# One order for VectorE and ScalarE through a whole MLP, and block products taken by pairs of tiles

## The chip, the core and the metric

The kernel runs on one core of one Trainium2 chip. The metric is the device time of one execution in microseconds (us), taken as the median of several runs. All engine names are those of the profile: PE is the matrix engine TensorE, PEld its weight loads, DVE is VectorE, ACT is ScalarE, POOL is GpSimd, and SP is the engine that issues most transfers (DMAs).

## What is computed

One layer of a hybrid decoder on a sequence of 512 tokens with 1024 channels, in float32. Three token mixers come first (an attention, a pooling and a gated MLP), then an output projection, a norm and a residual. The change touches only what follows them, the channel MLP:

```python
h = rms_norm(x, g_ff_pre[l])
ff = jnp.square(jax.nn.relu(h @ w_ff_in[l])) @ w_ff_out[l]     # 1024 -> 4096 -> 1024
x = x + rms_norm(ff, g_ff_post[l])
```

## The kernel before

**Precision.** Every matrix operand is held as a high and a low part. ACT casts the high part, DVE subtracts it from the original to get the low part, and PE makes three matmuls of each product: high by high, low by high, high by low. A weight arrives as a chunk of 128x1024 in a buffer `raw` (three of them), ACT casts it to `whi`, DVE writes `wlo` (six of each). `split_chunk` (L188) does this for one chunk, and starts the load of the chunk that is three further on. A `Weights` object (L232) calls it when a product asks for a weight: it makes all chunks ready up to three ahead of the one asked for.

**The MLP** goes through the 4096 hidden channels in four blocks (`b`, L961) of 1024. In each block, `ff_in` makes eight hidden tiles of 128 channels by 512 tokens (tile `accf`, 24 matmuls each), and `ff_act` (L898) takes ReLU (`rl`) and square (`ec`) on ACT, splits them (`ah`, `al`) and, for every second hidden tile, makes four more sums (`ec<-ec`, DVE) and splits those too; that second split is put off until `rest()` (L893) is called, by the next `ff_act` or ahead of the products.

**The products.** The second matrix product of the block is made by a scheme that needs seven products of half-size blocks instead of eight, in four stages named s2, s1, s3 and s4. Tokens come in four tiles t of 128; p is 0 or 1, and tiles p and 2 + p make a pair. M = 4 counts the pairs of hidden tiles. The banks of PSUM are `accy` (stage s2, and the product with the part A22), `accx` (A11, then AN, then AS, added up one on the other) and `accz` (AQ, then AR), each for p = 0 and 1. `gather` (L933) adds a bank to the result `ys` on DVE (in the first block the first such step of each `ys` is a copy on ACT). `accx` is gathered after A11, after AN, and after AS; since the next part is added in the same bank, PE can't go on there until DVE has read it. The weights of s1, s3 and s4 are sums of blocks of `w_ff_out`, which DVE makes in `block_sums` (L217) ahead of the cast. Four chunks make up each of s1, s3 and s4, and two s2; a chunk of s1, s3 or s4 feeds twelve matmuls.

In the three blocks that aren't the last, s3 first makes all of AN and gathers it, then all of AS, and s4 takes AR and A22 by turns. The last block goes by token tiles so that tiles finish one after another: each is scaled (`scaled_out`, L941), its squares are summed on ACT (`junk`), and `finish_out` (L948) multiplies it by its norm factor, adds the residual `x1b`, and stores it. For token tile 2 ACT and POOL do this (`pool=True`).

**What sets the order.** `InOrder` (L80) wraps an engine. While its flag `on` is true, each instruction is tied to the one before it on that engine, so the engine runs them as the program emits them. While it is false, a scheduler chooses the order by its own estimate of times. PE and SP go through the wrapper as well; PE is always tied. L982 switches DVE and ACT to the scheduler early in the first block, L1077 switches them back shortly before the end.

Of the kernel before, what the change touches and what calls it, by code (L numbers as in the profile page):

```python
# [48 lines left out]
def trunk_layer(ctx: ExitStack, tc: tile.TileContext, x, w_in, w_pool, pool_scale, gm_gain,  # L49
# [108 lines left out]
    NB = 4  # L158
    FT = FF // P // NB
    for b in range(NB):  # L160
        for f in range(0, FT, 2):
            use["f1", b, f] = plan_cols(ff_in_k, (b * FT + f) * P)


        for stage in ("s2", "s1", "s3", "s4"):
            use[stage, b] = range(len(plan), len(plan) + (2 if stage == "s2" else FT // 2))
            for m in range(0, FT // 2, 2 if stage == "s2" else 1):
                b11, b12, b21, b22 = (
                    ff_out_k[:, b * FT + 2 * m + o:b * FT + 2 * m + o + 1, c:c + 512]
                    for o in range(2) for c in (0, 512))  # L170
                if stage == "s2":
                    plan.append([ff_out_k[:, b * FT + 2 * m + 1:b * FT + 2 * m + 4:2, :512]])
                else:
                    plan.append({"s1": [b11, b12], "s3": [b22, b12], "s4": [b22, b21]}[stage])
                    derive[len(plan) - 1] = (stage, m)

    loaded, made = [], []

# [38 lines left out]
    def block_sums(raw, stage, m):  # L217

        one, two = raw[:, :512], raw[:, 512:]
        if stage == "s1":  # L220
            t1s[m] = ff.tile([P, T], F32, name="t1", bufs=4)
            dve.tensor_add(t1s[m], one, two)
            return [one, t1s[m]]
        if stage == "s3":

            dve.tensor_add(t1s[m], t1s[m], one)
            dve.tensor_add(two, two, one)
            return [t1s[m], two]
        dve.tensor_add(two, two, t1s[m])
        return [raw]  # L230

    class Weights:  # L232
# [697 lines left out]
    def block(which, p):  # L930
        return psum.tile([P, T], F32, name="acc" + which, tag=which, bufs=2)
# [13 lines left out]
            yg[t][hf] = slot("tmp", "yg") if t == LAST else ys[t][hf]  # L945
        dve.tensor_mul(yg[t][hf][:, c], ys[t][hf][:, c], gfpost[hf][:, c])

    def finish_out(t, r, g, c=WHOLE, queue=None, pool=False):  # L948

        rows = slice(t * P, (t + 1) * P)  # L950
        at = slice(g * T + c.start, g * T + c.stop)
        y = yg[t][g][:, c]
        if pool:
            act.activation(y, y, AF.Copy, scale=r)
            nc.gpsimd.tensor_add(y, y, x1b[t][:, at])
        else:
            dve.scalar_tensor_tensor(y, y, r, x1b[t][:, at], ALU.mult, ALU.add)
        (queue or nc.sync).dma_start(o2[rows, at], y)

    M = FT // 2  # L960
    for b in range(NB):  # L961
        first = 0
        if b == 0:

            first = 4
            halves = slice(0, T // 2), slice(T // 2, T)
            wks = [Weights(("f1", b, f), ahead=2 - f) for f in (0, 2)]
            pss = [bank4("mm", f, "psf") for f in range(first)]
            for f in range(first):
                ff_in(pss[f], wks[f // 2], f % 2, halves[0],  # L970
                      (lambda f=f: turn(f)) if f >= 2 else None)
            early.close()
            ff = ctx.enter_context(tc.tile_pool(name="ff", bufs=1, reuse_waits="tile"))
            home[0] = ff
            RINGS["tmp"] = 4
            gfpost = bcast_row(g_ff_post[0], [ff.tile([P, T], F32, name=f"gfpost{g}")
                                              for g in range(2)])
            Weights(("f1", b, first), ahead=2)[0]
            for f in range(first):
                ff_in(pss[f], wks[f // 2], f % 2, halves[1])  # L980
                ff_act(f, pss[f])
            act.on = dve.on = False  # L982
            banks.close()
            psum = ctx.enter_context(tc.tile_pool(name="psum2", bufs=1, space=PSUM,
                                                  reuse_waits="tile"))
            z = [block("z", p) for p in range(2)]
        for f in range(first, FT):
            if f % 2 == 0:
                wk = Weights(("f1", b, f))
            ps = block("f", f)  # L990
            ff_in(ps, wk, f % 2, slice(0, T))
            ff_act(f, ps)
        final = b == NB - 1
        if final:
            for i in range(2):
                pair = ff.tile([P, 2, D], F32, name="x1b", tag="ec", bufs=2)
                for t in (2 * i, 2 * i + 1):
                    x1b[t] = pair[:, t - 2 * i, :]
                    sp.dma_start(x1b[t], x1d[t])

        def stage(name, n, keep=False):

            wk = Weights((name, b), keep=keep)
            wk.tiles = [(i, j, k) for i in use[name, b] for j in range(len(plan[i]))
                        for k in range(plan[i][j].shape[1])]
            return lambda m, j: tile_of(wk, m * n + j)

        def tile_of(wk, i):
            i, j, k = wk.tiles[i]
            wk.ready(i)  # L1010
            h, l = made[i][j]
            return h[:, k, :], l[:, k, :]

        two = range(2)

        stagger = (0, 0), (0, 1), (1, 0), (0, 2), (1, 1), (0, 3), (1, 2), (1, 3)
        y = [block("y", p) for p in two]
        x = [block("x", p) for p in two]
        if b:
            z = [block("z", p) for p in two]  # L1020
        w2, w1 = stage("s2", 1, True), stage("s1", 2)
        def first(m, j):
            for p in two:
                product((x, z)[j][p], (A11, AQ)[j], p, m, w1(m, j))

        rest()
        for m in range(M):
            if m == M - 1:

                first(0, 0)  # L1030
                first(0, 1)
            for p in two:
                product(y[p], A12, p, m, w2(m, 0))
        for p in two:
            gather(2 + p, 0, y[p], ALU.add, b)
        for m, j in (1, 0), (1, 1), (2, 0), (3, 0), (2, 1), (3, 1):
            first(m, j)
            if (m, j) == (3, 0):
                for p in two:
                    gather(2 + p, 0, x[p], ALU.add, b)  # L1040
        if final:
            for p in two:
                scaled_out(2 + p, 0)
        for p in two:
            gather(p, 1, z[p], ALU.add, b)
        w = stage("s3", 2, True)
        for p, m in stagger:
            product(x[p], AN, p, m, w(m, 0), False)
            if m == M - 1:
                gather(2 + p, 1, x[p], ALU.subtract, b)  # L1050
        for p in two:
            for m in range(M):
                product(x[p], AS, p, m, w(m, 1), False)
            gather(p, 1, x[p], ALU.subtract, b)
            gather(p, 0, x[p], ALU.add, b)
        y = [block("y", p) for p in two]
        w = stage("s4", 2, final)
        if not final:
            for m in range(M):
                for j, ps, part in (0, z, AR), (1, y, A22):  # L1060
                    for p in two:
                        product(ps[p], part, p, m, w(m, j), j == 1)
            for p in two:
                gather(2 + p, 1, z[p], ALU.add, b)
                gather(p, 0, y[p], ALU.add, b)
            continue
        for p in two:
            scaled_out(p, 1)
        r = {}
        for p, m in stagger:  # L1070
            product(z[p], AR, p, m, w(m, 0), False)
            if m == M - 1:
                gather(2 + p, 1, z[p], ALU.add, b)
                scaled_out(2 + p, 1)
                r[2 + p] = post_r(2 + p)

        act.on = dve.on = True  # L1077
        for m in range(M):
            product(y[0], A22, 0, m, w(m, 1), True)
        gather(0, 0, y[0], ALU.add, b)  # L1080
        scaled_out(0, 0)
        for g in two:
            finish_out(2, r[2], g, pool=True)
        r[0] = post_r(0)
        finish_out(3, r[3], 1)
        for c in HALVES:
            ps = block("f", 0) if c.start else y[1]
            for m in range(M):
                product(ps, A22, 1, m, w(m, 1), True, c)
            gather(1, 0, ps, ALU.add, b, c)  # L1090
            scaled_out(1, 0, c)
        finish_out(3, r[3], 0)
        r[1] = rstd_d(twos[1], "p")
        for g in two:
            finish_out(0, r[0], g)
        finish_out(1, r[1], 1, queue=nc.scalar)
        finish_out(1, r[1], 0, HALVES[0])
        finish_out(1, r[1], 0, HALVES[1], queue=nc.scalar)


_INS = ["x", "w_in", "w_pool", "pool_scale", "gm_gain", "w_spatial", "b_spatial", "w_br_sb",
# [26 lines left out]
```

## Time and profile before

| what | value |
|---|---|
| median of 3 runs | 726.25 us (725.29 to 728.44) |
| the profiled execution's own time | 729.78 us |
| its span, first to last instruction | 728.0 us |
| PE busy | 703.2 us, 97% of the span |
| DVE busy | 495.4 us, 68% |
| ACT busy | 355.1 us, 49% |

The profiled execution is 3.5 us above the median and 1.8 us longer than its span. Busy time tells which engine has the most to do; what a change is worth is told by which engine waits for which, and where.

### The profile page before, as it was taken

To read this page: it belongs to the slowest core of one execution; us is meant where nothing else is said; L and a number is where in the kernel's file an instruction comes from. 1 tells how busy PE (TensorE), PEld (TensorE's weight loads), DVE (VectorE), ACT (ScalarE), POOL (GpSimd) and SP (SyncE) were. 2 spreads that over 40 slices of the span, in tenths; PEclk is the share of its full clock that TensorE was granted. 3 is DMA by queue.
4 is the path that set the end of the run, shared out by engine and by line. 5 is a ranking of instruction groups with operands and counts; after the bars stand their busy time and mean duration, and the time that the engine had idled before them with its cause. 6 is when DMAs were issued, how large, how long until landed. Compare 5 with 4: busy or idle time off the path is not lost.

```text
span 728.0 us, 9146 instructions
## 1 busy us (share of the span) xinstructions
PE 703.2 (97%) x3320; PEld 580.3 (80%) x3320; DVE 495.4 (68%) x769; ACT 355.1 (49%) x595; POOL 57.5 (8%) x108
## 2 busy tenths in 40 slices
PE   7999999999999999999999998999999999999984
PEld 4889887787888888888899776888878887888863
DVE  6745799777777444342676776656975678757876
ACT  6566656655544333321456564455434553455522
POOL 4100222111121000000030000000000000000003
PEclk9999999999999999999999999999999999999997
DMA  7272312322224332261336334732456225633623
GB/s 273 77 209 83 115 59 59 91 77 66 87 58 145 90 113 88 91 227 59 115 91 200 115 99 133 228 104 86 144 177 187 86 88 175 206 112 108 203 95 116
DMA packets 72431, 89.80 MB, mean 123 GB/s; under 512 B 4545, under 2 KB 49729, under 8 KB 72386
## 3 DMA queue, kind: packets, MB, share of 16 engines
q1 hardware_dynamic: 72096, 88.82, 39.3%
q8 instruction: 26, 0.43, 0.3%
q10 hardware_dynamic: 290, 0.40, 0.1%
q14 instruction: 19, 0.16, 0.1%
HBM read 85.01 MB, written 4.19 MB: 123 GB/s over the span
## 4 chain that ended last, share of the span: by engine, by line
PE 74%; DVE 13%; DMA 8%; ACT 2%; issue 2%; SPq 0%; POOL 0%; DVEq 0%; ACTq 0%; POOLq 0%
PE psc L90 26%; PE accf L90 16%; DMA raw<-in_w_ff_out_dram 7%; PE psb L90 6%; PE acc L90 6%; PE accx L90 4%; DVE wlo L90 3%; PE psv L90 3%; PE accz L90 3%; PE accy L90 3%; DVE ys L90 2%; PE psgv L90 2%; DVE raw L90 1%; PE z L90 1%; DVE t L90 1%
## 5 line engine op out<-in xcount | busy, mean ns | idle before, releaser
L90 DVE TENSOR_TENSOR wlo<-raw,whi 128x1024 fp32r<-128x1024 f32 (+1 forms) x145 | 159.1, 1101 | 106.8 <-ACT whi L90 106.1
L90 ACT CAST whi<-raw 128x1024 fp32r<-128x1024 f32 (+1 forms) x152 | 139.4, 927 | 141.2 <-PE psc L90 31.1
L90 PE MATMUL psc<-hT,whi 128*128 128x512 f32 x576 | 182.1, 397 | 0.0
L90 PE MATMUL accf<-hT,whi 128*128 128x512 f32 x448 | 138.1, 389 | 1.8 <-ACT rl L90 1.8
L90 PEld LDWEIGHTS psc<-hT,whi 128*128 128x128 f32 x576 | 103.8, 188 | 21.0 <-issue 1.5
L90 PE MATMUL psc<-hT,wlo 128*128 128x512 f32 x288 | 112.5, 391 | 0.0
L90 PEld LDWEIGHTS accf<-hT,whi 128*128 128x128 f32 x448 | 83.9, 188 | 19.6 <-ACT rl L90 2.2
L90 PE MATMUL accf<-hT,wlo 128*128 128x512 f32 x224 | 87.1, 389 | 0.0
L90 PEld LDWEIGHTS psc<-hT,wlo 128*128 128x128 f32 x288 | 54.1, 188 | 11.7
L90 PEld LDWEIGHTS accf<-hT,wlo 128*128 128x128 f32 x224 | 42.0, 188 | 8.7
L90 ACT CAST ah<-ec 128x768 fp32r<-128x768 f32 (+1 forms) x32 | 30.2, 944 | 37.6 <-DVE ec L90 37.1
L90 PE MATMUL accx<-whi,ah 128*128 128x512 f32 x96 | 39.1, 408 | 6.5 <-DVE ys L90 6.5
L284 POOL TENSOR_TENSOR pr<-pv,mhalf 128x1 f32<-128x1 f32 x8 | 5.6, 699 | 471.6 <-DVE pv L90 471.6
L90 PE MATMUL accx<-whi,al 128*128 128x512 f32 x96 | 38.8, 404 | 0.0
L90 PE MATMUL accx<-wlo,ah 128*128 128x512 f32 x96 | 38.7, 403 | 0.0
L90 DVE TENSOR_TENSOR al<-ec,ah 128x768 fp32r<-128x768 f32 (+1 forms) x32 | 34.8, 1088 | 4.5 <-ACT ah L90 4.5
L90 DVE TENSOR_TENSOR_SCAN nb<-nb,zeros 128x128 f32<-128x128 f32 (+3 forms) x32 | 27.5, 863 | 7.5 <-POOL nb L482 7.1
L90 DVE TENSOR_TENSOR ec<-ec 128x256 f32<-128x256 f32 x64 | 26.7, 421 | 7.2 <-ACT ec L90 6.9
L90 PEld LDWEIGHTS accx<-whi,ah 128*128 128x128 f32 x96 | 18.9, 197 | 12.6 <-DVE ys L90 8.6
L90 ACT CAST whi<-t 128x512 fp32r<-128x512 f32 x32 | 19.7, 617 | 14.7 <-PE accz L90 6.9
L90 ACT CAST a<-pt 128x128 fp32r<-128x128 f32 (+3 forms) x32 | 13.6, 426 | 25.9 <-PE pt L90 25.8
L90 ACT ACTIVATE sg<-psc 128x512 f32<-128x512 f32 x24 | 14.3, 597 | 22.7 <-PE psc L90 22.7
(199 smaller groups left out, 1251.7 us busy)
## 6 DMA issues: line engine op xcount, KB each, us to landing
raw<-in_w_ff_out_dram SPq DMA_DIRECT2D x96, 256.0 KB, 3.2
raw<-in_w_in_dram SPq DMA_DIRECT2D x42, 512.0 KB, 3.8
raw<-in_w_ff_in_dram SPq DMA_DIRECT2D x32, 512.0 KB, 3.9
xt<-in_x_dram SPq DMA_DIRECT2D x16, 256.0 KB, 5.8
raw<-in_w_out_dram SPq DMA_DIRECT2D x8, 512.0 KB, 3.7
raw<-in_w_ff_out_dram SPq DMA_DIRECT2D x8, 512.0 KB, 4.6
raw<-in_w_br_sb_dram SPq DMA_DIRECT2D x4, 512.0 KB, 3.5
x1d<-xt SPq DMA_DIRECT2D x8, 256.0 KB, 2.8
```

The costliest lines, as they stand in the source:

```text
L90: i = op(*args, **kw).ins
L284: nc.gpsimd.tensor_tensor(r, v, mhalf, ALU.pow)
```

## The change

Three things change, all in the MLP.

1. The two lines that switch the wrapper's flag off and on again are gone, so DVE and ACT keep the order of the program from the output projection to the end.
2. In the first three blocks, s3 takes A22 (`accy`) and AN (`accx`) by turns, and s4 takes AR (`accz`) and AS (`accx`) by turns, always two tiles p at a time. The blocks of weights move between the stages to fit, and in s3 both halves of a chunk are now summed in place and cast in one instruction of 128x1024 instead of two of 128x512. The number of sums is the same.
3. In the last block the two store steps of token tile 2 move from ACT and POOL to DVE, the last steps are in another order, and all weights of s4 are asked for before its first product.

```diff
-                    plan.append({"s1": [b11, b12], "s3": [b22, b12], "s4": [b22, b21]}[stage])
-                    derive[len(plan) - 1] = (stage, m)
+                    kind = stage + "f" * (b == NB - 1 and stage != "s1")
+                    plan.append({"s1": [b11, b12], "s3": [b22, b21], "s4": [b12, b22],
+                                 "s3f": [b22, b12], "s4f": [b22, b21]}[kind])
+                    derive[len(plan) - 1] = (kind, m)
...
         if stage == "s3":
+            dve.tensor_add(one, one, t1s[m])
+            dve.tensor_add(two, two, one)
+        elif stage == "s4":
+            dve.tensor_add(one, one, two)
+        elif stage == "s3f":
             dve.tensor_add(t1s[m], t1s[m], one)
             dve.tensor_add(two, two, one)
             return [t1s[m], two]
-        dve.tensor_add(two, two, t1s[m])
+        else:
+            dve.tensor_add(two, two, t1s[m])
         return [raw]
...
-            act.on = dve.on = False
...
+        if not final:
+            w = stage("s3", 2)
+            for m in range(M):
+                for j, ps, part in ((0, x, AN), (1, y, A22))[::1 if m == M - 1 else -1]:
+                    for p in two:
+                        product(ps[p], part, p, m, w(m, j), j == 1)
+                    if m == M - 1:
+                        for p in two:
+                            gather(*((p, 0, y[p], ALU.add, b) if j else
+                                     (2 + p, 1, x[p], ALU.subtract, b)))
+            w = stage("s4", 2)
+            for m in range(M):
+                for j, ps, part in (1, z, AR), (0, x, AS):
+                    for p in two:
+                        product(ps[p], part, p, m, w(m, j), False)
+            for p in two:
+                gather(2 + p, 1, z[p], ALU.add, b)
+            for p in two:
+                gather(p, 1, x[p], ALU.subtract, b)
+                gather(p, 0, x[p], ALU.add, b)
+            continue
...
-        w = stage("s4", 2, final)
-        if not final:
-            for m in range(M):
-                for j, ps, part in (0, z, AR), (1, y, A22):
-                    for p in two:
-                        product(ps[p], part, p, m, w(m, j), j == 1)
-            for p in two:
-                gather(2 + p, 1, z[p], ALU.add, b)
-                gather(p, 0, y[p], ALU.add, b)
-            continue
+        w = stage("s4", 2, True)
+        for m in range(M):
+            w(m, 0)
...
-        act.on = dve.on = True
         for m in range(M):
             product(y[0], A22, 0, m, w(m, 1), True)
         gather(0, 0, y[0], ALU.add, b)
+        finish_out(2, r[2], 0)
         scaled_out(0, 0)
-        for g in two:
-            finish_out(2, r[2], g, pool=True)
```

How the instructions of DVE move is seen at three places, all in the second block; the third block reads the same. The names are tiles with their numbers: `raw` a chunk, `t1` the running sum of two blocks of weights, `ec` and `al` hidden tiles, `ys` the result.

The first place is where the block's last hidden tiles (`ec_4663` before, `ec_4655` after) meet the first chunks of s1. On DVE before:

```order
L90 TENSOR_TENSOR wlo_4641<-raw_4544,whi_4640 128x512
L90 TENSOR_TENSOR wlo_4641<-t1_4642,whi_4640 128x512
L90 TENSOR_TENSOR wlo_4714<-raw_4563,whi_4713 128x512
L90 TENSOR_TENSOR wlo_4714<-t1_4715,whi_4713 128x512
L90 TENSOR_TENSOR t1_4755<-raw_4648 128x512
L90 TENSOR_TENSOR ec_4578<-ec_4578 128x256 x2
L90 TENSOR_TENSOR al_4613<-ec_4578,ah_4612 128x768
L90 TENSOR_TENSOR t1_4642<-t1_4642,raw_4721 128x512
L90 TENSOR_TENSOR ec_4578<-ec_4578 128x256
L90 TENSOR_TENSOR raw_4721<-raw_4721 128x512
L90 TENSOR_TENSOR al_4613<-ec_4578,ah_4612 128x1024
L90 TENSOR_TENSOR ec_4663<-ec_4663 128x256
```

On DVE after:

```order
L90 TENSOR_TENSOR t1_4634<-raw_4536 128x512
L90 TENSOR_TENSOR wlo_4633<-raw_4536,whi_4632 128x512
L90 TENSOR_TENSOR wlo_4633<-t1_4634,whi_4632 128x512
L90 TENSOR_TENSOR al_4605<-ec_4570,ah_4604 128x1024
L90 TENSOR_TENSOR al_4690<-ec_4655,ah_4689 128x768
L90 TENSOR_TENSOR ec_4655<-ec_4655 128x256 x4
L90 TENSOR_TENSOR al_4690<-ec_4655,ah_4689 128x1024
L90 TENSOR_TENSOR t1_4707<-raw_4555 128x512
L90 TENSOR_TENSOR wlo_4706<-raw_4555,whi_4705 128x512
L90 TENSOR_TENSOR wlo_4706<-t1_4707,whi_4705 128x512
L90 TENSOR_TENSOR t1_4730<-raw_4617 128x512
L90 TENSOR_TENSOR wlo_4729<-raw_4617,whi_4728 128x512
```

Before, the second chunk of s1 (`wlo_4714`) and sums for later chunks stand ahead of the last hidden tiles; after, the second chunk (`wlo_4706`) stands behind both splits of the last hidden tiles.

The second place is the start of s3, up to the gather that frees `accx` for AN. On DVE before:

```order
L90 TENSOR_TENSOR wlo_4785<-t1_4642,whi_4784 128x512
L90 TENSOR_TENSOR raw_4761<-raw_4761 128x512
L90 TENSOR_TENSOR wlo_4785<-raw_4721,whi_4784 128x512
L90 TENSOR_TENSOR ec_4663<-ec_4663 128x256
L90 TENSOR_TENSOR ys_4134<-ys_4134,accy_4705 128x512
L90 TENSOR_TENSOR wlo_4808<-t1_4715,whi_4807 128x512
L90 TENSOR_TENSOR wlo_4808<-raw_4744,whi_4807 128x512
L90 TENSOR_TENSOR ys_4136<-ys_4136,accy_4706 128x512
L90 TENSOR_TENSOR al_4698<-ec_4663,ah_4697 128x1024
```

On DVE after:

```order
L90 TENSOR_TENSOR ys_4136<-ys_4136,accy_4698 128x512
L90 TENSOR_TENSOR raw_4713<-raw_4713,t1_4634 128x512
L90 TENSOR_TENSOR raw_4713<-raw_4713 128x512
L90 TENSOR_TENSOR wlo_4777<-raw_4713,whi_4776 128x1024
L90 TENSOR_TENSOR raw_4736<-raw_4736,t1_4707 128x512
L90 TENSOR_TENSOR raw_4736<-raw_4736 128x512
L90 TENSOR_TENSOR wlo_4798<-raw_4736,whi_4797 128x1024
L90 TENSOR_TENSOR raw_4753<-raw_4753,t1_4730 128x512
L90 TENSOR_TENSOR raw_4753<-raw_4753 128x512
L90 TENSOR_TENSOR wlo_4813<-raw_4753,whi_4812 128x1024
L90 TENSOR_TENSOR ys_4134<-ys_4134,accx_4699 128x512
```

Before, other work stands between a chunk's sums and its `wlo`; after, each chunk's two sums are followed by its own `wlo`, and the first gather of `accx` comes behind three chunks of s3.

The third place is the gather that frees `accx` for AS. On DVE before:

```order
L90 TENSOR_TENSOR raw_4832<-raw_4832,t1_4715 128x512
L90 TENSOR_TENSOR raw_4865<-raw_4865,t1_4738 128x512
L90 TENSOR_TENSOR ys_4257<-ys_4257,accx_4707 128x512
L90 TENSOR_TENSOR wlo_4886<-raw_4832,whi_4885 128x1024
L90 TENSOR_TENSOR raw_4876<-raw_4876,t1_4755 128x512
L90 TENSOR_TENSOR ys_4265<-ys_4265,accx_4708 128x512
```

On DVE after:

```order
L90 TENSOR_TENSOR wlo_4846<-raw_4782,whi_4845 128x1024
L90 TENSOR_TENSOR raw_4803<-raw_4803 128x512
L90 TENSOR_TENSOR wlo_4867<-raw_4803,whi_4866 128x1024
L90 TENSOR_TENSOR raw_4818<-raw_4818 128x512
L90 TENSOR_TENSOR wlo_4887<-raw_4818,whi_4886 128x1024
L90 TENSOR_TENSOR raw_4851<-raw_4851 128x512
L90 TENSOR_TENSOR wlo_4906<-raw_4851,whi_4905 128x1024
L90 TENSOR_TENSOR ys_4282<-ys_4282,accx_4699 128x512
L90 TENSOR_TENSOR ys_4284<-ys_4284,accx_4700 128x512
L90 TENSOR_TENSOR ys_4292<-ys_4292,accy_4843 128x512
```

After, the fourth chunk of s3 (`wlo_4846`) and three chunks of s4 stand ahead of this gather; before, it stood between single steps of the s4 chunks.

## Rows read from the trace of the kernel before

**Rows 1.** The page: the span.

```profile
span 728.0 us, 9146 instructions
```

**Rows 2.** Windows: length, busy PE, PEld, DVE, ACT, POOL (count), clock, DMA share, GB/s.

```profile
421.80:465.40 43.60, 40.30 (x169) 32.55 (x169) 30.22 (x42) 23.08 (x34) 0.00 (x0) 0.96 0.48 146
465.40:508.90 43.50, 43.50 (x193) 36.04 (x192) 28.23 (x41) 23.02 (x32) 0.00 (x0) 1.00 0.39 121
508.90:547.70 38.80, 38.44 (x170) 31.49 (x169) 32.09 (x46) 16.97 (x23) 0.00 (x0) 1.00 0.54 163
...
591.20:630.40 39.20, 38.73 (x170) 31.37 (x169) 32.29 (x46) 17.37 (x23) 0.00 (x0) 1.00 0.53 163
...
673.90:717.30 43.40, 40.33 (x181) 33.12 (x179) 34.77 (x57) 18.76 (x34) 1.77 (x3) 0.96 0.36 121
717.30:728.00 10.70, 0.00 (x0) 0.00 (x0) 7.20 (x15) 1.02 (x4) 3.93 (x4) 0.61 0.52 196
```

**Rows 3.** Waits of PE in the MLP: for whom, us in total, times, longest.

```profile
PE accx L90 <- DVE ys L90: 6.5, 5, 3.0
PE accf L90 <- ACT rl L90: 1.8, 1, 1.8
```

**Rows 4.** Timeline of DVE, second block's products: start, duration, instruction, idle before.

```profile
512.79 0.95 DVE L90 TENSOR_TENSOR al<-ec,ah 128x768 fp32r<-128x768 f32 x1
...
514.26 0.42 DVE L90 TENSOR_TENSOR ec<-ec 128x256 f32<-128x256 f32 x1
514.60 0.69 DVE L90 TENSOR_TENSOR wlo<-t,whi 128x512 fp32r<-128x512 f32 x1
...
519.14 1.22 DVE L90 TENSOR_TENSOR al<-ec,ah 128x1024 fp32r<-128x1024 f32 x1
...
523.89 1.28 DVE L90 TENSOR_TENSOR ys<-ys,accx 128x512 f32<-128x512 f32 x2
```

**Rows 5.** Timelines of ACT and DVE: hidden tiles' chain, and sum to cast.

```profile
503.68 1.06 ACT L90 CAST ah<-ec 128x1024 fp32r<-128x1024 f32 x1 [2.49 <-DVE ec L90]
...
509.95 0.59 ACT L90 ACTIVATE rl<-accf 128x512 f32<-128x512 f32 x1
...
511.24 0.84 ACT L90 CAST ah<-ec 128x768 fp32r<-128x768 f32 x1
511.98 0.61 ACT L90 CAST whi<-t 128x512 fp32r<-128x512 f32 x1
...
694.11 1.05 ACT L90 CAST whi<-raw 128x1024 fp32r<-128x1024 f32 x1 [2.73 <-DVE raw L90]
...
504.77 1.23 DVE L90 TENSOR_TENSOR al<-ec,ah 128x1024 fp32r<-128x1024 f32 x1 [0.52 <-ACT ah L90]
...
693.34 0.69 DVE L90 TENSOR_TENSOR raw<-raw,t 128x512 f32<-128x512 f32 x1 [1.51 <-DMA raw<-in_w_ff_out_dram]
```

**Rows 6.** Timelines of DVE and PE at the longest wait, last block.

```profile
697.49 0.68 DVE L90 TENSOR_TENSOR raw<-raw,t 128x512 f32<-128x512 f32 x1
698.09 0.68 DVE L90 TENSOR_TENSOR ys<-ys,accx 128x512 f32<-128x512 f32 x1
...
698.82 0.54 PE L90 MATMUL accx<-whi,ah 128*128 128x512 f32 x1 [3.00 <-DVE ys L90]
```

**Rows 7.** Windows behind the 1.8 us wait and the 3.0 us wait, columns as in rows 2.

```profile
410.80:414.00 3.20, 3.17 (x14) 2.64 (x15) 3.12 (x6) 3.19 (x6) 0.00 (x0) 1.00 0.07 23
...
699.20:702.60 3.40, 3.40 (x10) 2.63 (x9) 1.99 (x3) 0.00 (x0) 0.00 (x0) 0.51 0.32 122
```

**Rows 8.** Loads of `w_ff_out` chunks (median us to landing), and of `x1b`.

```profile
raw<-in_w_ff_out_dram SPq DMA_DIRECT2D x96, 256.0 KB, 3.2
...
DMA to landing us min/median/max: 5.2/6.0/6.9
```

**Rows 9.** Timelines of DVE and POOL behind the last matmul.

```profile
719.71 1.04 DVE L90 TENSOR_TENSOR yg<-ys,gfpost 128x256 f32<-128x256 f32 x1
...
718.93 1.53 POOL L955 TENSOR_TENSOR ys<-ys,x1b 128x512 f32<-128x512 f32 x1
```

More of the change, by code (lines that the diff above doesn't have):

```diff
@@ L946, in scaled_out, with finish_out @@
         dve.tensor_mul(yg[t][hf][:, c], ys[t][hf][:, c], gfpost[hf][:, c])
-    def finish_out(t, r, g, c=WHOLE, queue=None, pool=False):
+    def finish_out(t, r, g, c=WHOLE, queue=None):
         rows = slice(t * P, (t + 1) * P)
@@ L952, in finish_out @@
         y = yg[t][g][:, c]
[L953 to L957, printed above, removed]
+        dve.scalar_tensor_tensor(y, y, r, x1b[t][:, at], ALU.mult, ALU.add)
         (queue or nc.sync).dma_start(o2[rows, at], y)
@@ L1040, in trunk_layer @@
                     gather(2 + p, 0, x[p], ALU.add, b)
-        if final:
-            for p in two:
-                scaled_out(2 + p, 0)
         for p in two:
             gather(p, 1, z[p], ALU.add, b)
+        y = [block("y", p) for p in two]
+        if not final:
[19 more added lines that the diff above has]
+            continue
+        for p in two:
+            scaled_out(2 + p, 0)
         w = stage("s3", 2, True)
@@ L1055, in trunk_layer @@
             gather(p, 0, x[p], ALU.add, b)
-        y = [block("y", p) for p in two]
-        w = stage("s4", 2, final)
-        if not final:
-            for m in range(M):
-                for j, ps, part in (0, z, AR), (1, y, A22):
-                    for p in two:
-                        product(ps[p], part, p, m, w(m, j), j == 1)
-            for p in two:
-                gather(2 + p, 1, z[p], ALU.add, b)
-                gather(p, 0, y[p], ALU.add, b)
-            continue
+        w = stage("s4", 2, True)
+        for m in range(M):
+            w(m, 0)
         for p in two:
@@ L1074, in trunk_layer @@
                 scaled_out(2 + p, 1)
-                r[2 + p] = post_r(2 + p)
-        act.on = dve.on = True
+        for p in two:
+            r[2 + p] = post_r(2 + p)
         for m in range(M):
@@ L1080, in trunk_layer @@
         gather(0, 0, y[0], ALU.add, b)
+        finish_out(2, r[2], 0)
         scaled_out(0, 0)
-        for g in two:
-            finish_out(2, r[2], g, pool=True)
-        r[0] = post_r(0)
-        finish_out(3, r[3], 1)
         for c in HALVES:
@@ L1089, in trunk_layer @@
                 product(ps, A22, 1, m, w(m, 1), True, c)
+            if c.start:
+                finish_out(2, r[2], 1)
             gather(1, 0, ps, ALU.add, b, c)
             scaled_out(1, 0, c)
+            if not c.start:
+                r[0] = post_r(0)
         finish_out(3, r[3], 0)
         r[1] = rstd_d(twos[1], "p")
[L1094 to L1098, printed above, removed]
+        finish_out(3, r[3], 1)
+        finish_out(0, r[0], 1)
+        finish_out(0, r[0], 0, queue=nc.scalar)
+        finish_out(1, r[1], 1)
+        finish_out(1, r[1], 0, HALVES[0], queue=nc.scalar)
+        finish_out(1, r[1], 0, HALVES[1])
 _INS = ["x", "w_in", "w_pool", "pool_scale", "gm_gain", "w_spatial", "b_spatial", "w_br_sb",
```

## The prediction, made before the changed kernel ran

> **What bounds the kernel now.** I read the MLP by stages first. The hidden tiles of a block take 43.5 us for 192 matmuls with PE busy throughout, 0.2266 us a matmul; the 168 matmuls of a product stage should then take 38.1. The four product stages take 43.6, 38.8, 39.2 and 43.4 [rows 2], so the two in the middle are within about 1 us of PE's pace. The waits say what is lost: 6.5 us in five waits of `accx` for a gather, and 1.8 for a ReLU [rows 3]. At the longest one DVE was not idle: a sum for a later chunk stood ahead of the gather, and PE started 0.05 us after the gather's end [rows 6]. Behind that 3.0 us wait PE ran 3.4 us at a granted clock of 0.51, the 1.2 GHz level, a loss of 3.4 x 0.49 = 1.7; behind the 1.8 us wait it stayed at 1.00 [rows 7]. That happened twice (both outer stages show 0.96 [rows 2]). So at most 8.3 + 3.3 = 11.6 us can come back from PE's waits, in 726.
>
> DVE is the engine to look at, since it is busy for 32 of the middle stages' 39 us [rows 2]. What counts is when it reaches a gather.
>
> **What the change does to DVE: prices.** Back to back, DVE starts each instruction 0.08 before the last record ends (two gathers in 1.28 [rows 4]), so I count 0.60 for a sum, a gather or a 512-wide subtraction, 0.34 for an `ec` step, 0.87 and 1.14 for `al` 768 and 1024 wide, and 1.14 for a 1024-wide `wlo`, which has no row here and the same shape as that `al` [rows 4]. From the end of a sum to its cast 0.08 passes, from the end of a cast to DVE 0.03; casts take 0.61, 0.84 and 1.05 for 512, 768 and 1024 [rows 5].
>
> A chunk needs sums (DVE), cast (ACT), subtraction (DVE). In the scheduler's order other work fills DVE while ACT casts. In the program's order the next instruction on DVE is the subtraction that waits for this cast. A chunk of the new s3 then holds DVE for 0.60 + 0.69 + 0.08 + 1.05 + 0.03 + 1.14 = 3.59 us, one of s4 (one sum) for 2.99, one of s1 for 0.69 + 0.08 + 0.61 + 0.03 + 0.60 = 2.01. PE uses up a chunk in 12 x 0.2266 = 2.72. The single wide cast saves little: two subtractions are 1.20, one is 1.14. It also takes away an overlap, since with two casts the first subtraction can run under the second.
>
> The Trainium skill (Perfetto Trace Analysis, section Per-instruction lifecycle) says that ACT, DVE and GpSimd are strict FIFOs, so a ready gather can't pass a waiting subtraction. Rows 6 agree. By that rule the sum is the one below; without it a gather would go when its bank is ready, and the time would be that of rival 1.
>
> **The walk through block two.** Time 0 is the stage's first `accy` matmul.
> - The last hidden tiles come first now: ReLU at about 0.2 (estimate), 1.29 to the cast, 0.84, `al` 768 to 3.2, four sums to 4.7, cast 1024 to 5.8, `al` 1024 to 7.0 [rows 4, 5].
> - Chunks two to four of s1, 3 x 2.01, to 13.0, each just ahead of PE (8.2, 10.9 and 12.2). Two gathers of `accy`, 14.2.
> - Three chunks of s3, 3 x 3.59, to 25.0. Only then comes the gather of `accx`; PE may go on at 25.7. PE finished s1 (72 matmuls) at 16.3 and, with the first chunk ready at 17.8, `accy` at 19.1. It waits 6.6 us. Before, the same gather ran at 523.89 [rows 4], 15.0 after the stage's start.
> - Three more gathers to 27.4, the fourth chunk of s3 to 31.0, three of s4 to 40.0: behind these stands the gather that frees `accx` for AS, done at 40.7. PE had finished s3 and the first AR at 36.5, and waits 4.2.
> - Then 42 matmuls, 9.5: the stage ends at **50.2** instead of 38.8 (+11.4). Block three is the same: +11.0.
>
> A chunk's load takes 3.2 [rows 8] and a buffer is free two chunks, 6 us or more, ahead of its next use, so loads don't hold this up.
>
> Block one: its first gathers of `accy`, `accz` and (in s3) `accx` are copies on ACT. Three s3 chunks end at 23.8, two gathers 25.0, the fourth chunk 28.6, two s4 chunks 34.5; sum and cast of the third to 36.4 stand ahead of the copy on ACT, 37.0; plus 9.5 is 46.5 against 43.6: +2.9. Ahead of it, ACT's order no longer puts a cast before the ReLU that PE waited 1.8 for [rows 3]: -1.8.
>
> Block four keeps its stages. Its s3 chunks are still cast in halves (2.61 each), but start when `raw` has landed behind the 2 MB of `x1b`: 9.0 + 6.5 = 15.6 (median and maximum for `x1b` are 6.0 and 6.9 [rows 8]). Three chunks to 23.4, the `accx` gather 24.1, others and two scalings to 27.0, the fourth chunk 29.6, two s4 chunks 35.6, and only then the gather for AS, 36.4. AS of p = 0 to 39.1, p = 1 to 41.8, gathers to 43.1, and behind these, in order, the last two s4 chunks to 46.1 and 49.1. AR ends at 51.0; A22 (12 whole and 24 half-wide matmuls) takes 5.4: **56.5** against 43.4, +13.1.
>
> **The end.** The last 10.7 us have no matmul [rows 2]. A DVE step of 256 columns took 1.04 there while POOL ran its add [rows 9]; elsewhere such a step takes 0.42. Without POOL that goes, and two 512-wide steps come to DVE; in the new order I count 9.4 from the last matmul to the end: -1.3, bounds 0 and -3.
>
> **The clock.** Waits of 4 to 8 us come back in three stages in a place where PE is what everything then waits for; behind 3.0 us the loss was 1.7 [rows 7]. 3 x 1.7 = +5.0, bounds 0 (hidden) and what the rival below says.
>
> **Sum.** 2.9 - 1.8 + 11.4 + 11.0 + 13.1 - 1.3 + 5.0 = +40.3. The profiled execution took 729.78 for a span of 728.0 [rows 1] and would take 770; it lies 3.5 above the median, so the median goes to 726.25 + 40.3 = 766.5, say **766**.
>
> **Rivals.**
> 1. *The pairs cover the gathers, faster.* If DVE reached the first `accx` gather of each stage by 17.5, PE would never wait: 726.25 - 11.6 - 1.3 = 713. For it: DVE has 7 idle us in each middle stage [rows 2], and the new PE order puts 12 or more matmuls (2.7 us) between a bank's last part and the next in it. Against: it must come 7.5 us earlier than my walk, where 3 x 1.16 are cast waits and 7.0 the hidden tiles. Chance 0.05.
> 2. *The lead is kept.* If casts for the s1 chunks aren't held up by the last hidden tiles, the walk starts 4 to 5 us earlier in all four blocks and the clock mostly stays: 766 - 18 - 5 = 743. Against it is the order of DVE, where `al` 1024 stands ahead of the second s1 chunk. Chance 0.1.
> 3. *The clock stays low.* Waits now come with every chunk, each about 1 us with 2.5 us of work between. If PE ran at 1.2 GHz (0.427 a matmul) from the first gather of `accx` on, the 90 matmuls behind it would take 38.4 and block two end at 64; with the other stages likewise at 63, 64 and 68, that is 50 more than the sum, 816; half of that, 790. No row shows it: after 1.8 us the clock stayed. Chance 0.1. The Trainium skill (TensorE: Matmul & The Clock Gate, on a second failure mode, PSUM-queue cycling) describes just this, a clock that swings between its levels when a kernel's matmul groups are parted by short idle times; here only the two stretches behind some 3 us of idle show it so far.
> 4. *No change to measure*, within 0.5% (about what a measurement of this kernel can tell): gains and losses would have to cancel; 0.02.
>
> My own case has 0.73, and 752 to 782 for itself (each stage's start by 1 us either way, the end, the clock's 0 to 5 and some more). The range reaches into cases 2 and 3: 745 to 790. Faster by over 0.5% is 0.05, the same 0.02, slower 0.93.
>
> **What would show it.** In the changed trace: PE's waits for `ys` grow from 6.5 to some 35 us, nearly all at `accx`, two in each product stage; DVE's idle time with ACT's `whi` as releaser comes with each s3 and s4 chunk, about 1.1 us each; product stages take 46, 50, 50 and 56 us, hidden tiles stay at 43.5; the granted clock falls behind the long waits. I am wrong if the first `accx` gather of block two starts before 20 us into its stage, or if the stages stay below 42.

## The result, and the profile after

The changed kernel takes 771.0 us in the median of four runs (769.96 to 773.32); the kernel before takes 727.35 beside it (four runs, 725.29 to 729.44). The ratio is 1.0605, 95% interval 1.0561 to 1.0648. The forecast was 766, with a range of 745 to 790. The profiled execution took 771.9 for a span of 770.2, so the span grew by 42.2 against [rows 1].

The page of the kernel after: its span, then busy time, share and instructions of each engine.

```profile
span 770.2 us, 9105 instructions
PE 715.3 (93%) x3320; PEld 586.2 (76%) x3320; DVE 495.2 (64%) x759; ACT 352.9 (46%) x581; POOL 54.8 (7%) x106
```

DVE is as busy as before (495.2 and 495.4 us): its work is the same and comes later. PE has the same 3320 matmuls and is busy for 12.1 us more, as its granted clock is lower in the product stages (0.88 to 0.90 in the windows that follow, 0.96 to 1.00 in [rows 2]).

Windows of the kernel after, columns as in [rows 2]: the product stages of blocks one, two and four (that of block three takes 51.1 like that of two), one stage of hidden tiles, the end.

```profile
420.30:468.30 48.00, 41.52 (x169) 33.29 (x168) 32.27 (x42) 22.94 (x30) 0.00 (x0) 0.89 0.45 143
511.80:562.90 51.10, 41.81 (x169) 32.99 (x168) 34.94 (x47) 17.87 (x21) 0.00 (x0) 0.90 0.39 124
...
701.00:759.40 58.40, 44.08 (x181) 34.53 (x179) 40.96 (x66) 20.11 (x36) 1.06 (x2) 0.88 0.33 109
468.30:511.80 43.50, 43.50 (x193) 36.05 (x192) 23.47 (x33) 20.78 (x28) 0.00 (x0) 1.00 0.35 109
759.40:770.20 10.80, 0.00 (x0) 0.00 (x0) 7.28 (x18) 1.02 (x4) 1.85 (x2) 0.60 0.51 194
```

Against [rows 2] the product stages are 4.4, 12.3, 11.9 and 15.0 longer, 43.6 together; the hidden tiles keep their 43.5. DVE's time accounts for the 12.3 of the second stage: it is busy for 34.94 instead of 32.09 (+2.85) and idle for 16.16 instead of 6.71 (+9.45). The 2.85 is work that was done earlier before: in the hidden tiles ahead of it DVE is now busy for 23.47, where it was 28.23 [rows 2].

What DVE waits for in the second stage: first the kernel after (511.8 to 562.9), then, behind the dots, the kernel before in its own second stage (508.9 to 547.7).

```profile
DVE wlo L90 <- ACT whi L90: 9.7, 8, 1.2
DVE al L90 <- ACT ah L90: 3.8, 2, 2.7
...
DVE wlo L90 <- ACT whi L90: 5.2, 5, 1.4
```

In the hidden tiles ahead of it, 468.3 to 511.8, its waits are one row; behind the dots stand the waits of the kernel before for casts in its hidden tiles (465.4 to 508.9), where it also waited 2.8 us for loads:

```profile
DVE al L90 <- ACT ah L90: 19.5, 6, 8.2
...
DVE wlo L90 <- ACT whi L90: 8.9, 8, 1.9
DVE al L90 <- ACT ah L90: 0.5, 1, 0.5
```

So DVE stands 19.5 us at splits of hidden tiles while PE has plenty to do, and does no chunk work in that time; then it waits 9.7 us at eight casts of chunks while PE is short of them. PE's waits in the MLP, as in [rows 3]:

```profile
PE accx L90 <- DVE ys L90: 34.0, 7, 6.6
```

34.0 us for gathers of `accx` instead of 6.5; no other row of PE's waits in the MLP is over 1.5. The wait of 1.8 for `rl` is gone.

The timeline of DVE in the second stage, which answers to [rows 4] (start, duration, instruction, and in brackets the idle time ahead and for whom):

```profile
526.01 0.69 DVE L90 TENSOR_TENSOR raw<-raw,t 128x512 f32<-128x512 f32 x1
526.73 0.69 DVE L90 TENSOR_TENSOR raw<-raw 128x512 f32<-128x512 f32 x1
528.59 1.23 DVE L90 TENSOR_TENSOR wlo<-raw,whi 128x1024 fp32r<-128x1024 f32 x1 [1.16 <-ACT whi L90]
529.73 0.69 DVE L90 TENSOR_TENSOR raw<-raw,t 128x512 f32<-128x512 f32 x1
...
537.15 1.28 DVE L90 TENSOR_TENSOR ys<-ys,accx 128x512 f32<-128x512 f32 x2
...
552.52 1.28 DVE L90 TENSOR_TENSOR ys<-ys,accx 128x512 f32<-128x512 f32 x2
```

One chunk of s3 runs from 526.01 to 529.73, 3.72 us, with 1.16 of idle time at its own cast. The first gather of `accx` starts 537.15 - 511.8 = 25.3 into the stage (15.0 before, [rows 4]), the second at 40.7. PE, at those two gathers:

```profile
537.88 0.79 PE L90 MATMUL accx<-whi,ah 128*128 128x512 f32 x1 [6.58 <-DVE ys L90]
...
553.25 0.50 PE L90 MATMUL accx<-whi,ah 128*128 128x512 f32 x1 [1.77 <-DVE ys L90]
```

Windows of the kernel after behind these two waits, as in [rows 7]:

```profile
537.80:541.20 3.40, 3.32 (x8) 2.64 (x9) 3.12 (x6) 0.10 (x1) 0.00 (x0) 0.50 0.49 159
541.20:544.60 3.40, 3.40 (x13) 2.70 (x12) 1.83 (x2) 1.39 (x2) 0.00 (x0) 0.73 0.04 5
544.60:548.00 3.40, 3.40 (x17) 2.81 (x16) 1.83 (x2) 1.39 (x2) 0.00 (x0) 1.00 0.56 179
...
553.20:556.60 3.40, 3.35 (x15) 2.78 (x16) 2.40 (x4) 0.85 (x1) 0.00 (x0) 1.00 0.51 154
```

Behind the 6.58 us wait the granted clock is 0.50 (the 1.2 GHz level) and then 0.73, a loss of 3.4 x (0.50 + 0.27) = 2.6 us. But the bank that PE went to next wasn't free yet: PE came later to it than forecast and waited 1.77 there, not 4.2.

### The profile page after: what moved, and what is told of

Read it like the earlier page. It is cut to its first block, busy times and chain, and to the rows that moved or that the text cites. A ratio compares the mean times of both kernels' runs of the same rounds, so it can differ in the third digit from the quotient of the medians.

```text
span 770.2 us, 9105 instructions
## 1 busy us (share of the span) xinstructions
PE 715.3 (93%) x3320; PEld 586.2 (76%) x3320; DVE 495.2 (64%) x759; ACT 352.9 (46%) x581; POOL 54.8 (7%) x106
## 4 chain that ended last, share of the span: by engine, by line
PE 71%; DVE 13%; ACT 7%; issue 6%; POOL 1%; DMA 1%; ACTq 0%; DVEq 0%; SPq 0%; POOLq 0%
PE psc L90 23%; PE accf L90 20%; PE psb L90 6%; PE acc L90 5%; ACT whi L90 4%; PE accx L90 4%; DVE ys L90 3%; PE psv L90 3%; DVE raw L90 3%; PE accz L90 2%; PE psf L90 2%; DVE wlo L90 2%; PE psgv L90 1%; DVE t L90 1%; PE z L90 1%
## 5 line engine op out<-in xcount | busy, mean ns | idle before, releaser
L90 DVE TENSOR_TENSOR wlo<-raw,whi 128x1024 fp32r<-128x1024 f32 (+1 forms) x145 | 164.3, 1144 | 105.5 <-ACT whi L90 105.1
L90 ACT CAST whi<-raw 128x1024 fp32r<-128x1024 f32 (+1 forms) x152 | 143.3, 959 | 147.0 <-DVE raw L90 78.3
L90 PE MATMUL accx<-whi,ah 128*128 128x512 f32 x96 | 42.0, 438 | 34.0 <-DVE ys L90 34.0
L90 ACT ACTIVATE rl<-accf 128x512 f32<-128x512 f32 x28 | 16.7, 598 | 59.0 <-PE accf L90 59.0
L90 PE MATMUL accx<-wlo,ah 128*128 128x512 f32 x96 | 41.1, 428 | 0.0
L90 PE MATMUL accy<-wlo,ah 128*128 128x512 f32 (+1 forms) x64 | 26.3, 411 | 1.5 <-DVE wlo L90 1.5
L90 ACT CAST whi<-t 128x512 fp32r<-128x512 f32 x20 | 12.4, 622 | 31.2 <-DVE t L90 31.2
L90 PE MATMUL accz<-wlo,ah 128*128 128x512 f32 x64 | 25.1, 393 | 1.5 <-DVE wlo L90 1.5
```

The costliest lines, as they stand in the source:

```text
L90: i = op(*args, **kw).ins
```

## The experiments

The theory was: the program's order alone makes DVE pay for every cast, and the gathers that stand behind the chunks come late; pairs neither cause nor cure that. The rivals: the new order of PE and the blocks of weights cost the time; and, against a cure, that another wait takes the place of the one removed. Each ratio is to the kernel before on the same chip.

**1. The order alone (e1).** The stages and chunks of the kernel before, with only the two lines gone that give the order away and take it back; the last steps are those of the kernel before too.

```diff
-            act.on = dve.on = False
...
-        act.on = dve.on = True
```

> The kernel before with the order of the program kept on DVE and ACT through the MLP, and nothing else changed. Theory (the strict order alone costs the time): the same walk with the old stages gives product stages of 46 to 48, 51, 51 and 58 us, because AN still waits for a gather behind three s3 chunks and AS for one behind two s4 chunks; some 768 us. Rival (the pairs of tiles cost the time): within 5 us of 727.

Measured: 774.4 us, ratio 1.0737 (1.0705 to 1.0769). The four product stages take 46.4, 52.1, 52.3 and 60.1. The second one, and PE's main wait:

```profile
511.50:563.60 52.10, 42.53 (x170) 34.00 (x169) 36.31 (x53) 17.38 (x24) 0.00 (x0) 0.90 0.34 112
...
PE accx L90 <- DVE ys L90: 35.6, 7, 6.3
```

The order alone costs the whole loss, and some more than the full change (774.4 against 771.0 us, on different chips). It is also 6 us above my expectation: the last three stages take 1 to 2 us more each than I had put for them.

The chunks of s3 are cast in halves here and hold DVE for 2.64 us each (525.66 to 528.30), a little less than the 2.72 in which PE uses one up. Still the stage takes 52.1, since the gather of `accx` stands behind three of them, 22.1 into the stage, and PE, which goes from s1 straight to AN, waits 6.31 us for it. So a quick chunk isn't enough where a gather stands behind several.

**2. The pairs alone (e2).** The kernel after with the two lines put back, one early in the first block's hidden tiles, the other ahead of the last block's A22.

```diff
+            act.on = dve.on = False
...
+        act.on = dve.on = True
```

> The changed kernel with only the order given back to the scheduler from the first block's hidden tiles to shortly before the end. Theory: PE's waits at accx fall from 34 to under 5 us in all, product stages of 39 to 43 us; 720 to 728 us. Rival (the pairs cost the time): above 755 us.

Measured: 717.77 us against 721.99 for the kernel before, ratio 0.9945 (0.9928 to 0.9962), so a little faster. Its product stages (the third, left out, takes 38.7) and its end, and PE's waits:

```profile
420.10:458.90 38.80, 38.42 (x169) 31.46 (x169) 29.33 (x37) 22.39 (x29) 0.00 (x0) 1.00 0.55 178
502.40:540.50 38.10, 38.10 (x169) 31.53 (x169) 32.39 (x42) 17.54 (x19) 0.00 (x0) 1.00 0.58 189
...
666.20:705.90 39.70, 38.73 (x181) 31.94 (x179) 35.29 (x58) 17.71 (x33) 1.07 (x2) 1.00 0.38 136
705.90:715.60 9.70, 0.00 (x0) 0.00 (x0) 6.30 (x16) 0.82 (x4) 1.85 (x2) 0.66 0.50 191
...
PE accx L90 <- DVE ys L90: 1.6, 3, 1.0
```

In the second stage PE is busy for 38.10 of 38.10. The same chunks, the same wide casts, the same turns of banks; only the order on DVE and ACT differs. DVE's, ahead of the gather:

```profile
514.20 1.22 DVE L90 TENSOR_TENSOR wlo<-raw,whi 128x1024 fp32r<-128x1024 f32 x1
515.33 1.29 DVE L90 TENSOR_TENSOR raw<-raw 128x512 f32<-128x512 f32 x2
516.53 1.28 DVE L90 TENSOR_TENSOR ys<-ys,accx 128x512 f32<-128x512 f32 x2
517.73 1.22 DVE L90 TENSOR_TENSOR wlo<-raw,whi 128x1024 fp32r<-128x1024 f32 x1
```

No idle time between a sum and a subtraction, because two sums and two gathers stand there, and the gather comes at 516.53 - 502.4 = 14.1 instead of 25.3. The two lines free DVE and ACT together, and no run parts them; but in the second stage of the kernel after ACT starts the first cast of s3 0.08 us behind the sum (527.42 to 527.50), so there ACT's order doesn't hold the cast up. The stages add up to 9.7 us less than [rows 2], while the medians differ by only 4.2. The next run says part of why.

**3. The kernel before once more (e5), and the last steps alone (e6).** e5 is the kernel before, unchanged; e6 is it with only the last steps of the kernel after (token tile 2 finished on DVE):

```diff
-        for g in two:
-            finish_out(2, r[2], g, pool=True)
...
+        finish_out(2, r[2], 0)
...
+                finish_out(2, r[2], 1)
```

> The kernel before once more, for a trace on the chip on which it took 722 us and the pairs in free order 717.8. The trace of before that I have has outer product stages of 43.6 and 43.4 us, the one of the pairs 38.8 and 39.7, together 8 us, while the times differ by 4.2. Theory (part of it is the execution, not the kernel): one of the outer stages is 2 to 5 us shorter here, the span some 720. Rival (the stages are as in the trace I have, and something outside the MLP is shorter here): outer stages of 43 to 44 us again.

> The kernel before with the changed last steps alone (token tile 2 finished on DVE, not on ACT and POOL, and the new order of the stores). My count gave -1.3 us for them, the changed kernel's trace shows 10.8 us behind the last matmul as before. Theory (the gain is there, but the late s4 chunks of the strict order push DVE's work behind the last matmul and eat it): 9.5 to 9.8 us behind the last matmul, the time 1 us below before. Rival (two more steps on DVE cost what POOL's absence gives): 10.8 us and no change.

e5 took 725.2 in its one execution. Its first product stage (the fourth takes 41.9), and the stretch behind its longest wait of 3.25 us:

```profile
420.30:462.10 41.80, 38.71 (x170) 31.36 (x169) 29.04 (x41) 22.32 (x33) 0.00 (x0) 1.00 0.49 152
...
695.80:699.20 3.40, 3.36 (x15) 2.79 (x16) 2.69 (x4) 0.00 (x0) 0.00 (x0) 1.00 0.46 152
```

Here no clock fall followed, and the outer stages are 1.8 and 1.5 shorter than in [rows 2], a little less than the 2 to 5 that I had expected of one of them. The execution of [rows 2] had clock falls in these stages that this one hasn't (0.96 there, 1.00 here), so some 3.3 of e2's 9.7 is that. e6 took 727.97, ratio 1.0001 (0.9968 to 1.0035); its end is 9.7 instead of 10.7, which its median can't show.

**4. Two casts instead of one (e3).** The strict order kept, a chunk of s3 and s4 in two halves, so that the first subtraction runs under the second cast.

```diff
-        return [raw]
+        return [one, two] if stage in ("s3", "s4") else [raw]
```

> The changed kernel with the s3 and s4 chunks of the first three blocks cast and subtracted in two halves, so that the first subtraction runs under the second cast. Theory (DVE idles for each cast): a chunk holds DVE for 2.61 us, not 3.59 (s3) and 2.99 (s4), the first accx gather comes 2.9 us earlier, the wait ahead of AS goes; stages two and three 45.6 instead of 51.1, stage one 44.3 instead of 48.0; some 756.5 us. Rival (the waits come from where the gathers stand alone, the cast does not matter): more instructions on both engines and no gain, 771 us.

Measured: 756.96, ratio 1.0500 (1.0474 to 1.0526); the stages 45.1, 45.9, 45.9, 58.4, and 24.5 us of waits for `accx`. A chunk on DVE:

```profile
520.91 0.68 DVE L90 TENSOR_TENSOR raw<-raw,t 128x512 f32<-128x512 f32 x1
521.63 0.69 DVE L90 TENSOR_TENSOR raw<-raw 128x512 f32<-128x512 f32 x1
522.33 1.38 DVE L90 TENSOR_TENSOR wlo<-raw,whi 128x512 fp32r<-128x512 f32 x2
523.62 0.68 DVE L90 TENSOR_TENSOR raw<-raw,t 128x512 f32<-128x512 f32 x1
```

A chunk takes 2.71 instead of 3.72, with no idle time in it, and the second stage falls from 51.1 to 45.9. So the wide cast costs 5.2 us in this stage when the order is strict. Against e1's second stage, which has halves in s3 as well, 45.9 is 6.2 less; that comes with the pairs and with halves in s4, which no run parts. The fourth stage, already in halves for s3, stays at 58.4.

**5. The second chunk of s1 ahead of the last hidden tiles (e4).** The weights of a block's last two hidden tiles are asked for with five chunks ahead instead of three, so the second chunk of s1 comes one step earlier in DVE's order.

```diff
-                wk = Weights(("f1", b, f))
+                wk = Weights(("f1", b, f), ahead=5 if f == FT - 2 else AHEAD)
```

> The changed kernel with the second chunk of s1 prepared one step earlier, ahead of the block's last hidden tiles. Theory (DVE's chain from the last hidden tiles to the gather is what PE waits for): 2.0 us off that chain in each block, 769 - 6 to 8 = some 763.5 us, with the first accx wait at 4.6 instead of 6.6 us. Rival (the first wait is hidden by the second one): the first wait shrinks, the time stays within 2 us of 771.

Measured: 763.52, ratio 1.058 (1.055 to 1.061); the stages 45.6, 50.8, 49.1 and 56.5. In blocks two and three the gathers come 1.9 to 2.0 us earlier, as the theory has it. The first wait of `accx` didn't fall to the expected 4.6, it is 6.32 in both: PE too comes to that bank 1.6 us earlier, mainly because the first chunk of s3, for which it waited 0.17 and 0.77 us in the kernel after, is ready sooner. In block three the stage gains 2.0; in block two 0.3. There PE waited 2.67 at the second gather, and the windows behind it show a fall:

```profile
547.19 0.50 PE L90 MATMUL accx<-whi,ah 128*128 128x512 f32 x1 [2.67 <-DVE ys L90]
...
547.10:550.50 3.40, 3.31 (x11) 2.63 (x12) 2.43 (x5) 0.81 (x1) 0.00 (x0) 0.72 0.50 154
550.50:553.90 3.40, 3.40 (x13) 2.77 (x12) 3.13 (x3) 2.13 (x3) 0.00 (x0) 0.77 0.13 19
```

3.4 x (0.28 + 0.23) = 1.7 us: what the earlier gather brought went back to the clock. In block three the second wait was 2.06 us, and the clock stayed at 1.00 behind it.

**6. PE kept busy in its long waits (e7).** Idle matmuls into an unused bank ahead of AN and AS (24 ahead of each block's AN; 14 ahead of AS in blocks two and three, 20 in block four; 144 in all, not the 82 to 96 of the expectation); their results aren't used.

```diff
+        def keep_busy(n):
+            ps = block("f", 0)
+            hi = parts[0][0]
+            for _ in range(n):
+                pe.matmul(ps, lhsT=hi[:, 0, :P], rhs=..., start=True, stop=True)
```

> The changed kernel with 82 to 96 idle matmuls in all into an unused bank, 24 ahead of the first AN product of each block, 14 ahead of AS in blocks two and three, 20 ahead of AS in block four, so that PE works while it would wait and its clock should stay. Theory (the clock's fall is hidden in blocks two and three, since PE is early for the second gather anyway, and costs in blocks one and four): stage one 46.4 to 47 instead of 48.0, stages two and three within 0.5 of 51.1, stage four 56 to 56.5 instead of 58.4; some 4 us less than the changed kernel. My prediction's term had 1.7 us in each of blocks two to four. Rival (the clock is a main cost): 8 us or more, in all stages.

Measured: 768.22, ratio 1.0542 (1.0482 to 1.0602). Its first two product stages, and three short waits of PE in the fourth:

```profile
418.40:465.40 47.00, 44.55 (x194) 35.74 (x193) 30.25 (x39) 21.89 (x29) 0.00 (x0) 1.00 0.45 143
...
508.90:560.00 51.10, 48.01 (x208) 38.34 (x207) 34.94 (x47) 17.84 (x21) 0.00 (x0) 1.00 0.39 125
...
742.28 0.50 PE L90 MATMUL accz<-whi,ah 128*128 128x512 f32 x1 [1.14 <-ACT whi L90]
743.54 0.50 PE L90 MATMUL accz<-wlo,ah 128*128 128x512 f32 x1 [0.76 <-DVE wlo L90]
...
745.35 0.79 PE L90 MATMUL accz<-whi,ah 128*128 128x512 f32 x1 [0.25 <-ACT whi L90]
```

With the clock at 1.00 throughout, block two takes 51.1 as it did with a fall: the fall there cost nothing, DVE was the later one. Block one gains 1.0. In block four my expectation missed: the clock held through the long waits, and then fell behind two short ones. The matmuls behind 1.14 and 0.76 us are still quick; from 744.8 to 750.3 the granted clock is 0.50, and the waits of 0.25 and 0.47 us lie in that stretch. The stage stayed at 58.5. The kernel after has the same two waits at this place (1.14 and 0.76 us, at 747.38 and 748.64), and its clock stayed at 1.00 there.

**7. Chunks asked for one ahead instead of three (e8).** In s2, s1 and s3 of the first three blocks, so that a gather stands behind fewer chunks.

```diff
-            wk = Weights((name, b), keep=keep)
+            wk = Weights((name, b), keep=keep, ahead=AHEAD if final or name == "s4" else 1)
```

> The changed kernel with chunks of s2, s1 and s3 in the first three blocks made ready one ahead instead of three, so that in the program's order each accx gather stands behind one chunk and not three. Theory (DVE's chain of chunks with a cast wait in each is the bound, the gathers' place only decides which wait PE shows): the accx waits go in blocks one to three, waits for wlo take their place, and stages take 44, 49, 49 us; 8 to 9 us less than the changed kernel. Rival (the place of the gathers is the whole cost): stages of 40 us or less and 25 us or more.

Measured: 762.24, ratio 1.0464 (1.0405 to 1.0524); the stages 43.7, 49.6, 48.9, 57.7. PE's waits:

```profile
PE accx L90 <- DVE ys L90: 10.4, 2, 6.3
PE accy L90 <- ACT whi L90: 4.9, 3, 2.1
...
PE accy L90 <- DVE wlo L90: 3.6, 5, 0.8
```

The waits for `accx` fall from 34.0 to 10.4, all that is left being in the last block, and waits for `whi` and `wlo` take their place. The first three stages gain 4.3, 1.5 and 2.2 only. So with these wide chunks the place of the gather decides which wait is seen, and the pace of DVE's chunks decides how long the waits last altogether.

**8. The order given away later (e9).** As e2, with the first line behind the first block's hidden tiles, just ahead of the put-off split of the last one.

> The pairs in free order, with the order given free only from the first block's products on, so that its hidden tiles keep the order of the program, which took away the 1.3 to 1.8 us wait of accf for a ReLU in the changed kernel. Theory: the wait goes here too and nothing else moves, 1.4 us less than the pairs in free order, 0.992 to 0.993 of before. Rival (the scheduler used the first block's hidden tiles to bring s1 chunks forward, as it does in the later blocks): stage one grows by 2 us or more and takes the gain back, 0.995 or above.

Measured: 722.07, ratio 0.9935 (0.9910 to 0.9960). The wait of 1.3 for a ReLU that e2 has is gone, but others came:

```profile
PE accx L90 <- DVE ys L90: 2.7, 1, 2.7
PE accz L90 <- DVE al L90: 2.2, 1, 2.2
```

I had expected that nothing else moves; the first product stage is 40.6 where e2 has 38.8, and the fourth 43.1, with a clock fall, where e2 has 39.7. Its interval and that of e2 overlap; nothing is gained by it.

**9. The strict order mended as far as it goes (e10).** e3, e4 and e8 together.

> The changed kernel, order still strict, with all three single edits: halves of chunks, the second s1 chunk one step earlier, and one chunk ahead instead of three in s2, s1 and s3. Theory (with 2.61 us a chunk DVE keeps PE's 2.72, and the gathers stand where their bank is ready): stages one to three 40 to 41 us, the last one 56.5; 1.013 to 1.020 of before. Rival (strict order also costs in ways not in my walk): stages of 43 us or more, above 1.027.

Measured: 741.23, ratio 1.0190 (1.0162 to 1.0218). The first, second and fourth product stage:

```profile
418.10:456.70 38.60, 38.59 (x170) 31.36 (x169) 29.82 (x45) 21.37 (x35) 0.00 (x0) 1.00 0.47 146
...
500.20:542.40 42.20, 39.31 (x169) 31.33 (x168) 34.76 (x53) 17.23 (x27) 0.00 (x0) 1.00 0.41 131
...
671.80:728.50 56.70, 44.18 (x181) 34.71 (x179) 40.24 (x64) 19.31 (x35) 1.07 (x2) 0.91 0.33 110
```

The first block is at PE's pace now, the second 3.4 above its time in [rows 2]. In that stage the three edits together take off 8.9, more than the 7.0 that they take off when each is alone (5.2, 0.3 and 1.5). I had expected 40 to 41 for the first three stages; the third takes 42.4. Most of what is left is the last block, 13.3 above its time in [rows 2], where the three bring 1.7.

## Why the prediction was right, step by step

**The mechanism** was as forecast. e1 shows it without the pairs, e2 the pairs without it. PE's waits for gathers came to 34.0 us where some 35 were forecast, in seven waits and not eight: the second one of block one is for a copy on ACT, and PE didn't wait there. By the Trainium skill (Perfetto Trace Analysis, section Per-instruction lifecycle) DVE is a strict FIFO. The lines of the second stage agree: the gather of `accx` at 537.15 came behind three subtractions, for each of which DVE had waited 1.16 us.

**Chunk prices.** s3 was put at 3.59 and measured 3.72: the second sum reads what the first wrote and starts 0.72 behind it, where I had counted 0.60 for any instruction. s4 was put at 2.99 and measured 3.07 (543.32 to 546.39), with 1.24 of idle time where 1.16 was put.

**Block two and three.** First gather at 25.0 and first wait 6.6 forecast, 25.3 and 6.58 measured; second gather 40.0 and 40.7; the stage 50.2 and 51.1. The second wait was put at 4.2 and was 1.77, since PE ran slowly ahead of it; the end of the stage hung on DVE and didn't move (e7). So the walk without the clock is 0.9 short here, and with the clock's 1.7 it would be 0.8 too long.

**Block one** was mis-sized: 46.5 forecast, 48.0 measured. The chunks' 0.1 each are part of it, and e7 puts 1.0 on a clock fall that I hadn't put in this block: without the fall the stage takes 47.0, and PE waits 1.38 us for the copy on ACT there, as the walk has it.

**Block four:** 56.5 forecast, 58.4 measured. With the clock's 1.7 counted to it the forecast was 58.2. How the stage divides into DVE's lateness and the clock isn't shown, since e7's clock fell too.

**The clock** is the term of the sum that was wrong. I had 1.7 in each of blocks two to four, 5.0 in all. The falls came, but in two and three e7 shows that they cost nothing, because the loss is hidden behind DVE; in block one 1.0; in block four at most the 1.9 that the walk lacks there. That is 2.9 at most.

**The end** was put at -1.3 and stayed at 10.8. The edit does bring about 1.0: e2 and e6 end in 9.7, and the step of 1.04 us of [rows 9] takes 0.42 without the add on POOL. In the kernel after DVE is late there too: its first half-wide gather runs 0.3 us behind the start of the end (759.70), in e6 0.7 ahead of it. The ReLU's wait is gone, and the first product stage starts 1.5 us earlier, where -1.8 was forecast.

By the trace the four stages gave +43.6, where the forecast had 2.9 + 11.4 + 11.0 + 13.1 + 5.0 = 43.4. That the sum is right to 0.2 is luck: the four stages came out 5.2 above the walk (1.5, 0.9, 0.9 and 1.9), and a clock term of 5.0 filled that gap, though the clock cost 2.9 of it at most. The 1.4 missing at the end and 0.3 elsewhere make the 42.2 of the span, where 40.3 was forecast.

**The rivals.** The first, that pairs cover the gathers, needed the gather by 17.5; in the strict order it came at 25.3, and in e2 at 14.1, with 1.6 us of waits for `accx`. So its condition is met once the scheduler has the order; its price was too large, 13 us where e2 is 4.2 below the kernel before, and not all of that need be the pairs'. The second, a lead kept, did not come about; e4 shows that even a part of it moves the gathers as said. The third, a clock that stays low through a stage, did not come about: in the second stage it is at 1.00 again from 544.6 on, and no product stage of the kernel after has a mean under 0.88. The rule that I had set beside it (the Trainium skill, TensorE: Matmul & The Clock Gate, section A second HAM failure mode, on short idle times between matmul groups) has one piece of support here, the fall behind two short waits in e7. The same two waits in the kernel after had none.

**What stays open.** Whether e2's gain of 0.55% comes from the pairs, or in part from the last steps, isn't told apart by these runs: e6 bounds the latter at -0.3 to +0.35%. No run gives the order back to DVE alone or to ACT alone. And the last block in strict order wasn't mended.

## What to carry to other kernels

In a queue that runs in program order, a chunk of the form "sum here, cast on another engine, subtract here" holds the queue for its own work and for the other engine's too: 3.72 us here, 1.16 of it idle. Put that figure, not the busy share, against the consumer's pace (2.72); if it is larger, either split the chunk so that the halves overlap (2.71 here), or let other ready work stand in the gap. Look also at how many chunks stand ahead of the step that the consumer waits for: with chunks of 2.64 us e1 lost as much. And where a change reorders and restages at once, run each part alone: here the order alone cost 7%, and the rest without it brought 0.5%.

## What the runs showed of the hardware that wasn't expected

- The granted clock does not follow from the length of one wait. It fell behind waits of 6.58 us (kernel after) and 2.67 us (e4), and not behind one of 3.25 us (e5). In one execution of e6 it fell behind 2.45 us (0.66 over the next 3.4) and not behind 2.83 (1.00). In e7 it fell behind two waits of 1.14 and 0.76 us, after it had held at 1.00 through the longer waits that idle matmuls filled, and in the kernel after it didn't fall behind the same two.
- A fall cost more than the 1.7 us read before: behind the wait of 6.58 us the clock was 0.50 for 3.4 us and 0.73 over the next 3.4, a loss of 2.6.
- A slow clock cost nothing in one place. In block two of the kernel after PE lost 2.6 us and then still waited 1.77 for DVE; in e7, with the clock at 1.00, the stage takes the same 51.1.
- Two DVE instructions of 128x512 back to back start 0.60 apart (525.66 and 526.26 in e1), but 0.72 when the second reads what the first wrote (526.01 and 526.73 in the kernel after).
